# One ring of 40 rows, loads of eight rows and chains in fixed order, in a kernel that sums reciprocals

## The chip, the cores and the metric

The kernel runs on one core of one Trainium2 chip. The time is the device time of one execution in microseconds (us), as a median over several executions. Times inside a profile count from the start of its span, and the span is somewhat shorter than the measured time (172.6 against 175.2 us for the kernel before).

The engines are TensorE (PE in the profile; PEld is its weight load), VectorE (DVE), ScalarE (ACT), GpSimd (POOL) and SyncE (SP), which issues the DMAs.

## The reference

```python
x = np.abs(np.random.randn(32, 512, 1024)).astype(np.float32) + 1e-6
return np.sum(1.0 / x, axis=-1).astype(np.float32)
```

There are 16384 sums of 1024 reciprocals. With 128 partitions, each partition holds 128 "rows" of 1024 elements (4 KB); "a row" below means one row on all 128 partitions. All of x, 67.1 MB, has to be read once.

## The kernel before

The kernel takes reciprocals on ScalarE as exp(-ln x), and halves that work with an identity: for the two halves a and b of a row, 1/a + 1/b = (a + b) / (ab). So a product ab is made (512 elements), ScalarE takes Ln and Exp of it, and VectorE multiplies and sums. There are two ways to finish. In kind A VectorE multiplies both halves of the row by 1/(ab), a reduce over 1024 elements. In kind B TensorE first adds a + b into PSUM with an identity matrix, and VectorE reduces 512 elements only.

```python
A, B, C = (2, 0, GP, False), (2, 0, GP, True), (1, 1, GP, False)
GROUPS = (
    [A, B, A, B, C, B, A, B] * 7 + [A, B, A, B, A]
    + [(1, 0, GP, True), (1, 0, GP, False)] * 2
    + [(1, 0, GP, True), (1, 0, DV, True)]
)
...                                   # x tiles: 16 buffers of 2 rows
for np_, ns, eng, on_pe in GROUPS:
    xt = xpool.tile([P, n, D], f32, tag="xt")
    nc.sync.dma_start(out=xt, in_=x_v[:, c0 : c0 + n, :])
    eng.tensor_tensor(out=pr, in0=xt[:, :np_, :H], in1=xt[:, :np_, H:], op=mult)
    if on_pe:                         # kind B
        for j in range(np_):
            for h in range(2):
                nc.tensor.matmul(sm[:, j, :], lhsT=ident, rhs=xt[:, j, h*H:(h+1)*H],
                                 start=h == 0, stop=h == 1)
    ...                               # kind C: one row of two by ScalarE alone
    nc.scalar.activation(out=pr, in_=pr, func=Ln, scale=S)
    nc.scalar.activation(out=rc, in_=pr, func=Exp, scale=-1.0)
    for j in range(np_):
        nc.vector.tensor_tensor_reduce(out=row, in0=row, in1=rec, ..., accum_out=sums[...])
```

The order of the instructions on each engine is left to the scheduler of the framework. 64 of the 128 rows are of kind B.

Of the kernel before, what the change touches and what calls it, by code (L numbers as in the profile page):

```python
# [1 line left out]

# [6 lines left out]


@with_exitstack
def kernel(
    ctx: ExitStack,
    tc: tile.TileContext,
    x: bass.AP,
    out: bass.AP,
):








    nc = tc.nc
    f32 = mybir.dt.float32
    P = 128
    D = 1024
    H = D // 2  # L30
    F = 128

    S = float(2**17)



    GP, DV = nc.gpsimd, nc.vector
    A, B, C = (2, 0, GP, False), (2, 0, GP, True), (1, 1, GP, False)
    GROUPS = (
        [A, B, A, B, C, B, A, B] * 7  # L40
        + [A, B, A, B, A]
        + [(1, 0, GP, True), (1, 0, GP, False)] * 2
        + [(1, 0, GP, True), (1, 0, DV, True)]
    )

    Ln = mybir.ActivationFunctionType.Ln
    Exp = mybir.ActivationFunctionType.Exp
    mult = mybir.AluOpType.mult
    add = mybir.AluOpType.add

    x_v = x.flatten_outer_dims().rearrange("(p f) d -> p f d", p=P)
    out_v = out.flatten().rearrange("(p f) -> p f", p=P)

    act_sets = list(get_activation_tables(nc.m.arch).keys())
    nc.scalar.add_instruction(  # L55
        mybir.InstLoadActFuncSet(
            name=nc.get_next_instruction_name(),
            act_func_set_id=act_sets.index("natural_log_exp_and_others"),
            ins=[],
            outs=[],  # L60
        )
    )

    xpool = ctx.enter_context(tc.tile_pool(name="xpool", bufs=16))
    ppool = ctx.enter_context(tc.tile_pool(name="ppool", bufs=4))
    opool = ctx.enter_context(tc.tile_pool(name="opool", bufs=1))
    rpool = ctx.enter_context(
        tc.tile_pool(name="rpool", bufs=2, space=bass.MemoryType.PSUM)
    )

    spool = ctx.enter_context(
        tc.tile_pool(name="spool", bufs=2, space=bass.MemoryType.PSUM)
    )

    sums = opool.tile([P, F], f32)
    ident = opool.tile([P, P], f32)
    make_identity(nc, ident)

    c0 = 0
    for np_, ns, eng, on_pe in GROUPS:  # L80
        n = np_ + ns
        xt = xpool.tile([P, n, D], f32, tag="xt")
        nc.sync.dma_start(out=xt, in_=x_v[:, c0 : c0 + n, :])  # L83
        pr = ppool.tile([P, np_, H], f32, tag="pr")
        eng.tensor_tensor(out=pr, in0=xt[:, :np_, :H], in1=xt[:, :np_, H:], op=mult)  # L85
        if on_pe:
            sm = spool.tile([P, np_, H], f32, tag="sm")
            for j in range(np_):
                for h in range(2):
                    nc.tensor.matmul(  # L90
                        sm[:, j, :],
                        lhsT=ident,
                        rhs=xt[:, j, h * H : (h + 1) * H],
                        start=h == 0,
                        stop=h == 1,
                    )
        for j in range(np_, n):
            nc.scalar.activation(out=xt[:, j, :], in_=xt[:, j, :], func=Ln)  # L98
            nc.scalar.activation(  # L99
                out=xt[:, j, :],  # L100
                in_=xt[:, j, :],
                func=Exp,
                scale=-1.0,
                accum_out=sums[:, c0 + j : c0 + j + 1],
            )
        nc.scalar.activation(out=pr, in_=pr, func=Ln, scale=S)  # L106
        if on_pe:
            rc = pr
        else:
            rc = rpool.tile([P, np_, H], f32, tag="rc")  # L110
        nc.scalar.activation(out=rc, in_=pr, func=Exp, scale=-1.0)  # L111
        for j in range(np_):
            if on_pe:
                row, rec = rc[:, j, :], sm[:, j, :]
            else:
                row = xt[:, j, :].rearrange("p (h e) -> p h e", h=2)
                rec = rc[:, j, :].unsqueeze(1).to_broadcast([P, 2, H])
            nc.vector.tensor_tensor_reduce(  # L118
                out=row,
                in0=row,  # L120
                in1=rec,
                scale=S,
                scalar=0.0,
                op0=mult,
                op1=add,
                accum_out=sums[:, c0 + j : c0 + j + 1],
            )
        c0 += n
    assert c0 == F, c0

    nc.sync.dma_start(out=out_v, in_=sums)


# [1 line left out]
_INS = ['x']  # L135
_OUTS = [((32, 512), 'float32')]


# [23 lines left out]
```

## Time and profile before

The median is 175.2 us (174.65 to 175.26, three runs).

| engine | busy us of 172.6 | what it does |
|---|---|---|
| DMA | full from 4 to 160 us | loads of two rows, at the end one |
| GpSimd | 143.4 | 120 of 121 products (seven rows have none) |
| ScalarE | 142.0 | Ln and Exp |
| TensorE | 120.9 | sums of 64 rows |
| VectorE | 109.8 | reduces |

The prediction shows the lines. A line of a group gives count, busy time, mean duration in ns, and after the second bar the idle time before these instructions and what ended it.

### The profile page before, as it was taken

The numbers are of one execution on the slowest core, as the hardware profiler recorded it, in microseconds if no ns is written. First come the engines' busy times: TensorE is split into PE (matmuls) and PEld (weight loads), VectorE is DVE, ScalarE is ACT, GpSimd is POOL, SyncE is SP. The second block draws the span as 40 slices with busy tenths as digits, with TensorE's granted clock in tenths as the row PEclk, the third lists the DMA queues.
The fourth block names the chain that finished last, engine by engine and source line by source line (L and its number), as shares of the span: only waits on it lengthen the run. The fifth ranks groups of instructions, "written<-read, shape, count | busy, mean of one in ns | idle before, by whom it ended". The sixth has DMA issues, their size and how long they took to land.

```text
span 172.6 us, 1342 instructions
## 1 busy us (share of the span) xinstructions
PE 120.9 (70%) x256; PEld 47.4 (27%) x256; DVE 109.8 (64%) x243; ACT 142.0 (82%) x156; POOL 143.4 (83%) x72
## 2 busy tenths in 40 slices
PE   0099776767876767788666668977667876669480
PEld 0043322222332222233322223422222332223130
DVE  0009757874776757775578847468576755787791
ACT  2159989899878998889888996889988898988981
POOL 1599699969989799987999688997999979999920
PEclk9999999999999999999999996999999999999999
DMA  5999999999999999999999999999999999999500
GB/s 190 416 433 425 423 420 423 421 421 423 418 425 420 423 418 423 423 420 423 421 421 420 423 414 423 421 420 420 425 418 425 425 420 421 421 412 408 220 0 15
DMA packets 9799, 67.25 MB, mean 390 GB/s; under 512 B 1088, under 2 KB 1216, under 8 KB 1984
## 3 DMA queue, kind: packets, MB, share of 16 engines
q1 hardware_dynamic: 9792, 67.18, 94.0%
q8 instruction: 2, 0.03, 0.1%
q14 instruction: 5, 0.04, 0.1%
HBM read 67.11 MB, written 0.07 MB: 389 GB/s over the span
## 4 chain that ended last, share of the span: by engine, by line
DMA 78%; POOL 11%; ACT 2%; issue 2%; DVE 2%; SPq 1%; PE 1%; POOLq 0%; DVEq 0%
DMA xt<-in_x_dram 78%; POOL pr L85 11%; SPq L83 1%; ACT pr L106 1%; PE sm L90 1%; DVE xt L118 1%; ACT rc L111 1%; DVE pr L118 0%; ACT pr L111 0%; DVE pr L85 0%; POOLq L85 0%; DVE sums L118 0%; DVEq L118 0%; DVEq L157 0%
## 5 line engine op out<-in xcount | busy, mean ns | idle before, releaser
L85 POOL TENSOR_TENSOR pr<-xt 128x1024 f32<-128x1024 f32 (+1 forms) x66 | 142.7, 2166 | 21.1 <-DMA xt<-in_x_dram 15.2
L90 PE MATMUL sm<-xt,ident 128*128 128x512 f32 x256 | 120.9, 617 | 47.0 <-DMA xt<-in_x_dram 45.0
L118 DVE CUSTOM_DVE_ANT_1 xt<-xt,rc 128x1024 f32<-128x1024 f32 x57 | 67.7, 1219 | 50.2 <-issue 27.2
L106 ACT ACTIVATE pr<-pr 128x1024 f32<-128x1024 f32 (+1 forms) x67 | 65.0, 970 | 24.5 <-POOL pr L85 23.7
L90 PEld LDWEIGHTS sm<-xt,ident 128*128 128x128 f32 x256 | 47.4, 195 | 119.7 <-issue 57.8
L118 DVE CUSTOM_DVE_ANT_0 pr<-pr,sm 128x512 f32<-128x512 f32 x64 | 41.6, 685 | 9.8 <-ACT pr L111 8.6
L111 ACT ACTIVATE pr<-pr 128x1024 f32<-128x1024 f32 (+1 forms) x34 | 34.2, 1006 | 1.0
L111 ACT ACTIVATE rc<-pr 128x1024 f32<-128x1024 f32 (+1 forms) x33 | 29.9, 906 | 0.8
L118 DVE DVE_READ_ACCUMULATOR2_ANT sums<- 128x1 f32 x121 | 10.0, 82 | 0.0
L99 ACT ACTIVATE xt<-xt 128x1024 f32<-128x1024 f32 x7 | 7.3, 1041 | 0.0
L98 ACT ACTIVATE xt<-xt 128x1024 f32<-128x1024 f32 x7 | 7.3, 1040 | 0.0
L55 ACT ACT_TABLE_LOAD x1 | 1.3, 1283 | 0.7 <-PEq L146 0.7
L99 ACT ACTIVATION_READ_ACCUMULATOR xt<-xt 128x1 f32 x7 | 1.3, 186 | 0.0
L85 DVE TENSOR_TENSOR pr<-xt 128x512 f32<-128x512 f32 x1 | 0.7, 689 | 0.0
masks.py:197 POOL MEMSET ident<- 128x128 f32 x1 | 0.2, 204 | 0.3 <-POOLq L146 0.3
masks.py:199 POOL TENSOR_SCALAR_AFFINE_SELECT ident<-ident 128x128 f32<-128x128 f32 x1 | 0.3, 292 | 0.1
L146 POOL MEMSET const-float32-0.0<- 128x1 f32 x1 | 0.1, 98 | 0.2 <-issue 0.2
L146 POOL MEMSET const-bfloat16-1.0<- 128x1 bf16 x1 | 0.1, 101 | 0.0
L146 POOL MEMSET const-uint8-127<- 128x1 uint8 x1 | 0.1, 101 | 0.0
L146 POOL MEMSET const-float32-1.0<- 128x1 f32 x1 | 0.1, 98 | 0.0
## 6 DMA issues: line engine op xcount, KB each, us to landing
xt<-in_x_dram SPq DMA_DIRECT2D x61, 1024.0 KB, 19.8
xt<-in_x_dram SPq DMA_DIRECT2D x6, 512.0 KB, 15.6
out_dram<-sums SPq DMA_DIRECT2D x1, 64.0 KB, 1.5
```

The costliest lines, as they stand in the source:

```text
L55: nc.scalar.add_instruction(mybir.InstLoadActFuncSet(name=nc.get_next_instruction_name(), act_func_set_id=act_sets.index("natural_log_exp_ ...
L83: nc.sync.dma_start(out=xt, in_=x_v[:, c0 : c0 + n, :])
L85: eng.tensor_tensor(out=pr, in0=xt[:, :np_, :H], in1=xt[:, :np_, H:], op=mult)
L90: nc.tensor.matmul(sm[:, j, :], lhsT=ident, rhs=xt[:, j, h * H : (h + 1) * H], start=h == 0, stop=h == 1,)
L98: nc.scalar.activation(out=xt[:, j, :], in_=xt[:, j, :], func=Ln)
L99: nc.scalar.activation(out=xt[:, j, :], in_=xt[:, j, :], func=Exp, scale=-1.0, accum_out=sums[:, c0 + j : c0 + j + 1],)
L106: nc.scalar.activation(out=pr, in_=pr, func=Ln, scale=S)
L111: nc.scalar.activation(out=rc, in_=pr, func=Exp, scale=-1.0)
L118: nc.vector.tensor_tensor_reduce(out=row, in0=row, in1=rec, scale=S, scalar=0.0, op0=mult, op1=add, accum_out=sums[:, c0 + j : c0 + j + 1],)
L146: nc = _bacc.Bacc("TRN2", target_bir_lowering=False, num_devices=1)
```

## The change

The intent is to keep the stream of x denser (packets of 32 KB in place of 8 KB), to free GpSimd by giving 30 of the products to VectorE (GpSimd keeps 98 of 128, where it made 120), and to shorten the end by loads that shrink to one row. The order on every engine is fixed by hand. In the body a chain A of three rows and a chain B of four alternate; the last 30 rows are all of kind B. VectorE's products come in two kinds: for rows in V, TensorE copies one half into PSUM so that VectorE has one input only in SBUF; for rows in W, all in the tail, both inputs are in SBUF.

```diff
+    R = 40
+    LOADS = [8] * 11 + [5, 4, 3, 2, 5, 3, 3, 2, 3, 3, 1, 1, 2, 2, 1]
+    GROUPS = [(3, "A"), (4, "B")] * 14 + [(n, "B") for n in (4, 4, 4, 4, 4, 4, 3, 2, 1)]
+    V = {6 + 7 * i for i in range(14)} | {105, 108, 109}
+    W = {99, 101, 103, 104, 113, 115, 117, 118, 120, 121, 122, 123, 125}
...
+    ring = pool.tile([P, R, D], f32)
+    ps = pspool.tile([P, 8, H], f32)          # B: banks 0-3, A: 4-6, copies for V: 7
...
+    def product_v(g):
+        for r in range(g[0], g[0] + g[1]):
+            if r in V:
+                nc.tensor.matmul(ps[:, 7, :], lhsT=ident, rhs=xs(r, 1), start=True, stop=True)
+                b = ps[:, 7, :]
+            elif r in W:
+                b = xs(r, 1)
+            else:
+                continue
+            nc.vector.tensor_tensor(out=prod[:, p, :], in0=xs(r, 0), in1=b, op=mult)
...
+    with tc.manual_schedule():
+        for i, (r0, n, kind) in enumerate(chains):
+            ...                                # GpSimd's products of the chain
+            if kind == "A": rc = ps[:, 4 : 4 + n, :]
+            else:                              # B: two matmuls a row
+                tail = r0 >= 98
+                for j in range(n):
+                    bank[r0 + j] = nextb if tail else j
+                    for h in range(2): nc.tensor.matmul(ps[:, bank[r0 + j], :], ...)
+            nc.scalar.activation(out=pg, in_=pg, func=Ln, scale=S)
+            nc.scalar.activation(out=rc, in_=pg, func=Exp, scale=-1.0)
+            product_v(chains[i + 1])           # next chain's, before this one's reduces
+            ...                                # n reduces on VectorE
+            ahead(r0 + n)                      # loads for which the ring has room
```

More of the change, by code (lines that the diff above doesn't have):

```diff
@@ L31 @@
     F = 128
+    R = 40
+    NP = 20
     S = float(2**17)
-    GP, DV = nc.gpsimd, nc.vector
-    A, B, C = (2, 0, GP, False), (2, 0, GP, True), (1, 1, GP, False)
-    GROUPS = (
-        [A, B, A, B, C, B, A, B] * 7
-        + [A, B, A, B, A]
-        + [(1, 0, GP, True), (1, 0, GP, False)] * 2
-        + [(1, 0, GP, True), (1, 0, DV, True)]
-    )
+    LOADS = [8] * 11 + [5, 4, 3, 2, 5, 3, 3, 2, 3, 3, 1, 1, 2, 2, 1]
+    GROUPS = [(3, "A"), (4, "B")] * 14 + [(n, "B") for n in (4, 4, 4, 4, 4, 4, 3, 2, 1)]
+    V = {6 + 7 * i for i in range(14)} | {105, 108, 109}
+    W = {99, 101, 103, 104, 113, 115, 117, 118, 120, 121, 122, 123, 125}
     Ln = mybir.ActivationFunctionType.Ln
@@ L62 @@
     )
-    xpool = ctx.enter_context(tc.tile_pool(name="xpool", bufs=16))
-    ppool = ctx.enter_context(tc.tile_pool(name="ppool", bufs=4))
-    opool = ctx.enter_context(tc.tile_pool(name="opool", bufs=1))
-    rpool = ctx.enter_context(
-        tc.tile_pool(name="rpool", bufs=2, space=bass.MemoryType.PSUM)
-    )
-    spool = ctx.enter_context(
-        tc.tile_pool(name="spool", bufs=2, space=bass.MemoryType.PSUM)
-    )
-    sums = opool.tile([P, F], f32)
-    ident = opool.tile([P, P], f32)
@@ L77 @@
-    make_identity(nc, ident)
-    c0 = 0
-    for np_, ns, eng, on_pe in GROUPS:
-        n = np_ + ns
-        xt = xpool.tile([P, n, D], f32, tag="xt")
-        nc.sync.dma_start(out=xt, in_=x_v[:, c0 : c0 + n, :])
-        pr = ppool.tile([P, np_, H], f32, tag="pr")
-        eng.tensor_tensor(out=pr, in0=xt[:, :np_, :H], in1=xt[:, :np_, H:], op=mult)
-        if on_pe:
-            sm = spool.tile([P, np_, H], f32, tag="sm")
-            for j in range(np_):
-                for h in range(2):
-                    nc.tensor.matmul(
-                        sm[:, j, :],
-                        lhsT=ident,
-                        rhs=xt[:, j, h * H : (h + 1) * H],
-                        start=h == 0,
-                        stop=h == 1,
-                    )
-        for j in range(np_, n):
-            nc.scalar.activation(out=xt[:, j, :], in_=xt[:, j, :], func=Ln)
-            nc.scalar.activation(
-                out=xt[:, j, :],
-                in_=xt[:, j, :],
-                func=Exp,
-                scale=-1.0,
-                accum_out=sums[:, c0 + j : c0 + j + 1],
-            )
-        nc.scalar.activation(out=pr, in_=pr, func=Ln, scale=S)
-        if on_pe:
-            rc = pr
-        else:
-            rc = rpool.tile([P, np_, H], f32, tag="rc")
-        nc.scalar.activation(out=rc, in_=pr, func=Exp, scale=-1.0)
-        for j in range(np_):
-            if on_pe:
-                row, rec = rc[:, j, :], sm[:, j, :]
-            else:
-                row = xt[:, j, :].rearrange("p (h e) -> p h e", h=2)
-                rec = rc[:, j, :].unsqueeze(1).to_broadcast([P, 2, H])
-            nc.vector.tensor_tensor_reduce(
-                out=row,
-                in0=row,
-                in1=rec,
-                scale=S,
-                scalar=0.0,
-                op0=mult,
-                op1=add,
-                accum_out=sums[:, c0 + j : c0 + j + 1],
-            )
-        c0 += n
@@ L129, with load_one @@
-    assert c0 == F, c0
-    nc.sync.dma_start(out=out_v, in_=sums)
+    pool = ctx.enter_context(tc.tile_pool(name="pool", bufs=1))
+    pspool = ctx.enter_context(
+        tc.tile_pool(name="pspool", bufs=1, space=bass.MemoryType.PSUM)
+    )
+    ring = pool.tile([P, R, D], f32)
+    prod = pool.tile([P, NP, H], f32)
+    sums = pool.tile([P, F], f32)
+    ident = pool.tile([P, P], f32)
+    ps = pspool.tile([P, 8, H], f32)
+    loads = list(LOADS)
+    loaded = 0
+    def load_one():
+        nonlocal loaded
+        n = loads.pop(0)
+        r0 = loaded
+        a = r0 % R
+        m = min(n, R - a)
+        nc.sync.dma_start(out=ring[:, a : a + m, :], in_=x_v[:, r0 : r0 + m, :])
+        if m < n:
+            nc.sync.dma_start(
+                out=ring[:, 0 : n - m, :], in_=x_v[:, r0 + m : r0 + n, :]
+            )
+        loaded += n
@@ new lines, in need, with ahead @@
+    def need(r):
+        while loaded < r:
+            load_one()
+    def ahead(done):
+        while loads and loaded + loads[0] <= done + R:
+            load_one()
+    pslot = {}
+    nextp = 0
+    chains = []
+    r = 0
+    for n, kind in GROUPS:
+        if nextp + n > NP:
+            nextp = 0
+        for j in range(n):
+            pslot[r + j] = nextp + j
+        nextp = (nextp + n) % NP
+        chains.append((r, n, kind))
+        r += n
+    assert r == F and sum(LOADS) == F
@@ new lines, in xs, with pieces, product @@
+    def xs(r, h):
+        return ring[:, r % R, h * H : (h + 1) * H]
+    def pieces(r, n):
+        a = r % R
+        m = min(n, R - a)
+        return [(r, m)] + ([(r + m, n - m)] if m < n else [])
+    def product(r0, n):
+        for r, m in pieces(r0, n):
+            a, p = r % R, pslot[r]
+            nc.gpsimd.tensor_tensor(
+                out=prod[:, p : p + m, :],
+                in0=ring[:, a : a + m, :H],
+                in1=ring[:, a : a + m, H:],
+                op=mult,
+            )
@@ new lines, in product_v @@
+    def product_v(g):
+        for r in range(g[0], g[0] + g[1]):
+            p = pslot[r]
+            if r in V:
+                nc.tensor.matmul(
+                    ps[:, 7, :], lhsT=ident, rhs=xs(r, 1), start=True, stop=True
+                )
+                b = ps[:, 7, :]
[4 more added lines that the diff above has]
+            nc.vector.tensor_tensor(out=prod[:, p, :], in0=xs(r, 0), in1=b, op=mult)
+    make_identity(nc, ident)
@@ new lines @@
+    with tc.manual_schedule():
+        ahead(0)
+        product_v(chains[0])
+        nextb = 0
+        for i, (r0, n, kind) in enumerate(chains):
+            need(r0 + n)
+            r = a = r0
+            while r <= r0 + n:
+                if r == r0 + n or r in V or r in W:
+                    if r > a:
+                        product(a, r - a)
+                    a = r + 1
+                r += 1
+            p0 = pslot[r0]
+            pg = prod[:, p0 : p0 + n, :]
+            bank = {}
+            if kind == "A":
+                rc = ps[:, 4 : 4 + n, :]
+            else:
+                rc = pg
+                tail = r0 >= 98
+                for j in range(n):
+                    bank[r0 + j] = nextb if tail else j
+                    nextb = (nextb + 1) % 7 if tail else 0
+                    for h in range(2):
+                        nc.tensor.matmul(
+                            ps[:, bank[r0 + j], :],
+                            lhsT=ident,
+                            rhs=xs(r0 + j, h),
+                            start=h == 0,
+                            stop=h == 1,
+                        )
+            nc.scalar.activation(out=pg, in_=pg, func=Ln, scale=S)
+            nc.scalar.activation(out=rc, in_=pg, func=Exp, scale=-1.0)
+            if i + 1 < len(chains):
+                need(chains[i + 1][0] + chains[i + 1][1])
+                product_v(chains[i + 1])
+            for r in range(r0, r0 + n):
+                j = r - r0
+                if kind == "A":
+                    row = ring[:, r % R, :].rearrange("p (h e) -> p h e", h=2)
+                    rec = rc[:, j, :].unsqueeze(1).to_broadcast([P, 2, H])
+                else:
+                    row, rec = pg[:, j, :], ps[:, bank[r], :]
+                nc.vector.tensor_tensor_reduce(
+                    out=row,
+                    in0=row,
+                    in1=rec,
+                    scale=S,
+                    scalar=0.0,
+                    op0=mult,
+                    op1=add,
+                    accum_out=sums[:, r : r + 1],
+                )
+            ahead(r0 + n)
+        nc.sync.dma_start(out=out_v, in_=sums)
```

## The prediction

> **What bounds the kernel now.** I read the shares by slice first, because averages hide where an engine is full. In the page's second part each digit is the busy tenth of one 4.3 us slice:
>
> ```profile
> ACT  2159989899878998889888996889988898988981
> POOL 1599699969989799987999688997999979999920
> ...
> DMA  5999999999999999999999999999999999999500
> GB/s 190 416 433 425 423 420 423 421 421 423 418 425 420 423 418 423 423 420 423 421 421 420 423 414 423 421 420 420 425 418 425 425 420 421 421 412 408 220 0 15
> ```
>
> The DMA row has no gap between the second slice and the 37th: the stream of x is the bound of the body. GpSimd (POOL) and ScalarE (ACT) are close behind it. The rate falls in the last slices. The stretches say why:
>
> ```profile
> 0.00:4.00 4.00, 0.00 (x0) 0.00 (x0) 0.00 (x0) 1.28 (x1) 0.70 (x6) 1.00 0.55 172
> ...
> 60.00:80.00 20.00, 14.80 (x34) 5.87 (x33) 13.55 (x30) 17.74 (x20) 17.60 (x9) 1.00 1.01 422
> ...
> 155.00:160.00 5.00, 4.66 (x11) 1.59 (x9) 3.68 (x8) 4.22 (x5) 4.90 (x3) 1.00 1.02 408
> 160.00:165.00 5.00, 2.74 (x6) 1.17 (x7) 3.82 (x7) 4.88 (x8) 5.00 (x5) 1.00 0.42 164
> 165.00:170.00 5.00, 2.95 (x7) 0.87 (x5) 4.04 (x11) 3.18 (x6) 0.07 (x1) 1.00 0.00 0
> ```
>
> The columns are length, busy time of PE, PE's weight loads, VectorE (DVE), ACT and POOL, clock, DMA share, GB/s. The queues are full in both 60:80 and 155:160, but loads of two rows (8 KB to a partition) move 422 GB/s, the closing loads of one row (4 KB) only 408. The first stretch moved 172 x 4 = 0.69 MB, 1.6 us at 422, so bytes flow from about 2.4 us; the stretch 160:165 moved 0.82 MB, so they stop at about 162.0. Everything after that is tail. The chain that ended last says who fills it:
>
> ```profile
> 119.17 19.82 DMA xt<-in_x_dram
> ...
> 139.14 2.37 POOL pr L85
> ...
> 156.52 2.39 POOL pr L85
> 158.91 0.02 issue
> 158.93 1.07 ACT pr L106
> ...
> 169.09 0.69 DVE pr L118
> ```
>
> Up to 139 the chain is all loads; from 139 to 159 it is one GpSimd product after another: GpSimd is late by some microseconds when the stream ends, then ACT and VectorE work the rest off until 169.8. From there to the end of the span, 172.6, is the store of the sums and the close: 2.8 us. So before is start 2.4, stream 159.6, tail 7.8, close 2.8. The measured time is 175.2, 2.6 above the span, and I carry that 2.6 over.
>
> Costs of one instruction, from the groups kept apart by shape:
>
> ```profile
> L85 POOL TENSOR_TENSOR pr<-xt 128x1024 f32<-128x1024 f32 x54 | 127.6, 2365 | 20.3 <-DMA xt<-in_x_dram 15.0 <-ACT pr L106 1.1
> ...
> L106 ACT ACTIVATE pr<-pr 128x1024 f32<-128x1024 f32 x54 | 57.0, 1055 | 23.7 <-POOL pr L85 23.7
> ...
> L85 POOL TENSOR_TENSOR pr<-xt 128x512 f32<-128x512 f32 x12 | 15.1, 1273 | 0.7 <-DMA xt<-in_x_dram 0.2
> ...
> L106 ACT ACTIVATE pr<-pr 128x512 f32<-128x512 f32 x13 | 8.0, 615 | 0.8 <-DVE pr L85 0.8
> ```
>
> A product of GpSimd costs 181 ns and 1092 ns a row (2365 - 1273); an activation 175 ns and 440 ns a row. In the timeline VectorE starts its reduces 1.14 us apart where the row is the full one of 1024 (kind A), 0.61 us where it is 512 (kind B), and its own product takes 0.61 too.
>
> **What the Trainium skill says.** "DMA: Bandwidth & Descriptors", section "Specifications", gives 435 GB/s as the ceiling of the SBUF side; its section "Why small descriptors are slow" has a fixed overhead per packet inside the DMA engine. The trace agrees with both: 16 engines at 408 and 422 GB/s spend 160.6 ns on a 4 KB packet and 310.6 ns on an 8 KB one, so 150.0 ns for 4 KB and 10.6 ns fixed, which tends to 437 GB/s. "SBUF — State Buffer", section "Who interferes with whom": a VectorE instruction with two SBUF inputs and a GpSimd instruction that reads SBUF exclude one another, whichever started first runs to its end; with one SBUF input there is no conflict. That explains why 14 + 3 of the new products fetch one half through PE into PSUM. No line before shows the exclusion: the one VectorE product there runs at 167.0, when GpSimd has finished. "ScalarE: Activation LUTs", section "What ACT_TABLE_LOAD costs", has 186 ns + 0.833 ns an element, 1039 ns for 1024; the trace has 1055.
>
> **The change, part by part.**
>
> 1. Loads. 67 loads become 27 (26 in the list, of which rows 118 to 120 wrap round the ring and split). A load of n rows gives each of 16 engines 8 packets: n x 8 x 150.0 ns + 8 x 10.6 ns = 1.20 n + 0.085 us. Before: 128 x 1.20 + 67 x 0.085 = 159.3 us, which is the observed 159.6. After: 153.6 + 27 x 0.085 = 155.9. Gain 3.4 us, all of it on the path. Bytes would then end at 2.4 + 155.9 = 158.3. The first load of the kernel before was ready about 0.6 us after its bytes were due (5.5 against 2.4 + 2.5), so the last row is usable at 158.9.
>
> 2. The body. The first eight rows are usable only at 12.7 instead of the first two at 5.5. That costs nothing if the engines are faster than the stream. Seven rows (A of 3, B of 4) take the stream 8.5 us. GpSimd now makes six of the seven in two instructions of 0.18 + 3 x 1.09 = 3.46: 7.1 us with gaps, where it had almost no room. ACT: Ln and Exp of three rows 1.50 each, of four 1.94 each: 6.9. VectorE: 3 x 1.14 + 4 x 0.61 + 0.61 = 6.5. PE: 9 matmuls some 0.46 us apart, 4.1. All have 17% or more to spare. The seven rows whose sums ACT made alone are gone.
>
> 3. The ring. A load of eight needs the rows 40 before it released. Row 7 heads the third chain: its rows 8 and 9 land at 22.4, product to 25.9, Ln and Exp to 28.9, first reduce to 30.1. The sixth load can go then and is needed at 51.6, when the fifth ends. The second release comes at some 41 for 61. About 20 us are to spare, so the stream isn't starved.
>
> 4. The tail. I lay out the last chains with the landing time 3.0 + 1.20 rows + 0.085 loads. VectorE's order matters: the products of the next chain stand before the reduces of this one. Times in us; the third column is when the last product of the chain is ready:
>
> ```
> rows      landed  products  ACT to  reduces to
> 106-109   136.4   139.5     143.7   146.1
> 110-113   142.6   143.6     147.6   150.0
> 114-117   146.3   147.6     151.5   154.4
> 118-121   151.4   152.0     155.9   158.3
> 122-124   155.1   156.4     159.4   161.2
> 125-126   157.6   158.9     161.5   162.7
> 127       158.9   160.2     162.7   163.5
> ```
>
> For example 118-121: row 121 lands at 151.4, VectorE's product is done at 152.0, ACT needs 2 x 1.94, to 155.9, four reduces to 158.3. ACT then goes from chain to chain without a gap from 156.4: 3.0 + 2.1 + 1.25 for 3, 2 and 1 rows. To this I add 1.0 us as an estimate for the exclusion above: 113 beside the product of 110-112, 117 beside 116, 122/123 beside 124 and 125 beside 126 each may wait up to one GpSimd product, but some of it falls into waits that are there anyway. End of work 164.5, that is 5.6 after the last row instead of 7.2 (169.8 - 162.6).
>
> Sum: 164.5 + 2.8 = 167.3 span, + 2.6 = 169.9. Against 175.2 that is -5.3: 3.4 from packets, the rest from the tail. I put 169.8.
>
> **Rivals.** (a) Large packets don't pay: the rate stays 422 because something other than the packet cost sets it. For: the rate has been flat at 420 to 425 for 140 us, and only a stretch of 5 us shows 408. Against: the fit ends within half a per cent of the skill's ceiling, and the slice at 9 to 13 us shows 433. Then the loads end 3.4 later: 173.3, no change by the 2% rule. (b) The exclusion or VectorE's fixed order makes the tail the bound: a product that waits for a late row blocks the finished reduces behind it, and 13 products with two SBUF inputs take turns with GpSimd. VectorE has 3.1 to 4.3 us of work for each four rows against 4.9 of stream, so a wait of over 1 us per chain adds up. That would give back 2 to 4 us: 172 to 174. (c) The loads starve: if rows are released much later than in part 3, each eight-row load shows a gap in the DMA row. The 20 us speak against it; if it did happen at most of the 11 releases with 1 us each, 178 or more. (d) The tail is better than laid out, no exclusion felt: 168.5.
>
> **Range and chances.** Packets pay with some 75%; the tail is uncertain by 2 us either way. Main branch 168 to 172, rival (a) 172 to 174.5, (c) a few per cent above. The 2% lines are 171.7 and 178.7. So faster 0.71, same 0.25, slower 0.04; 167.3 to 173.2 should hold it 8 times in 10.
>
> **What will show it.** GB/s in the body should be 431 to 434, with no empty slice of DMA; if it is 420 to 425, step 1 is wrong. GpSimd should be busy for 98 products, near 112 us, and no longer a run of 20 us in the chain; the chain should be loads up to about 155 and then ACT and VectorE. The last load should land near 159 and work end near 164.5. VectorE's products in the tail with a mean well over 0.7 us, or products of GpSimd of one row well over 1.27, would show the exclusion. A chain with ring releases in it (a load waiting for VectorE) would make the prediction wrong upwards; so would a load lowered to packets of under 8 KB.

## More of the kernel before

One line that the prediction did not use, and should have, is TensorE's group (the view of groups of the kernel before, kept apart by shape):

```profile
L90 PE MATMUL sm<-xt,ident 128*128 128x512 f32 x256 | 120.9, 617 | 47.0 <-DMA xt<-in_x_dram 45.0 <-DVE sums L118 1.9
```

## The result

The changed kernel takes 197.07 us (196.77 to 197.23, four runs) against 174.93 of the kernel before in the same rounds. The ratio is 1.127, with a 95% interval of 1.124 to 1.130. A ratio here is the mean time of one kernel's fast runs over that of the other's of the same rounds, so it is not quite the ratio of the medians quoted. The prediction, 169.8 and faster with 71%, was wrong.

The second part of the page of the changed kernel, in slices of 4.9 us:

```profile
PE   0019988888896949999999989999999899999992
...
POOL 1029494999499949494949999994474244000000
...
DMA  6999999999999999999999999999999960000000
GB/s 222 430 430 430 437 437 444 430 437 430 445 430 430 427 437 430 430 430 430 437 425 430 403 423 425 427 434 411 415 428 411 424 271 0 2 3 0 0 0 13
```

The stream did what was hoped: no slice is empty, the rate is 427 to 445 up to 97 us where it was 416 to 433, and the bytes end in the 33rd slice, by estimate at about 159 us (271 / 424 of a slice that starts at 156). The last load is complete at 161.1 (landings and single records are read here from the kept trace, where no line is shown). GpSimd is done by 163. But TensorE is full to the end. The end of the chain that ended last reads (start, duration, what):

```profile
113.78 7.13 PE ps L161 x16
120.92 0.86 PE ps L124 x2
121.77 6.87 PE ps L161 x16
...
129.50 13.73 PE ps L161 x32
...
153.72 37.78 PE ps L161 x88
...
191.63 0.69 DVE prod L180
```

From 113.8 to 191.5 the chain is practically nothing but matmuls. L161 is the sum of a kind B row, L124 the copy for a V row. Sixteen records take 6.87 us, so one takes 0.43 us, and four B rows are sixteen records: four records a row. The piece of 32 records is rows 94 to 101; read record by record, the first one of row 98 starts at 136.2. The groups say the same:

```profile
L161 PE MATMUL ps<-ring,ident 128*128 128x512 f32 x344 | 151.1, 595 | 3.0 <-DVE sums L180 3.0
L124 PE MATMUL ps<-ring,ident 128*128 128x512 f32 x34 | 19.0, 642 | 21.6 <-DMA ring<-in_x_dram 20.8 <-DVE prod L132 0.8
```

The program issues 172 and 17 matmuls here; the trace has 344 and 34 records. Every matmul here, of 32-bit data, is two records. The line of the kernel before shows it as well: 256 records for 64 rows. The mean of 595 ns is longer than the 430 ns from start to start because matmuls overlap.

TensorE's account closes: 151.1 + 19.0 of busy time overlap to 166.9 us, idle time is 3.0 + 21.6, and the sum 191.5 is where the last matmul ends. Two stretches, before and after, show the body (columns as in the prediction):

```profile
60.00:100.00 40.00, 29.59 (x66) 11.66 (x65) 27.03 (x60) 35.55 (x39) 35.81 (x17) 1.00 1.01 422
```

```profile
60.00:100.00 40.00, 35.68 (x83) 15.41 (x82) 31.05 (x70) 30.29 (x20) 30.70 (x10) 1.00 1.00 431
```

ScalarE and GpSimd fell from 89 and 90% to 76 and 77%, as intended, and TensorE rose from 74% to 89%.

### The profile page after: what moved, and what is told of

Same layout as the page of the kernel before. It is cut to its first block, busy times and chain, and to the rows that moved or that the text cites. A ratio compares the mean times of both kernels' runs of the same rounds, so it can differ in the third digit from the quotient of the medians.

```text
span 195.0 us, 1440 instructions
## 1 busy us (share of the span) xinstructions
PE 166.9 (86%) x378; PEld 71.3 (37%) x378; DVE 123.5 (63%) x286; ACT 124.0 (64%) x75; POOL 114.6 (59%) x46
## 4 chain that ended last, share of the span: by engine, by line
DMA 45%; PE 40%; POOL 7%; issue 3%; DVE 2%; ACT 1%; SPq 0%; POOLq 0%; DVEq 0%; ACTq 0%
DMA ring<-in_x_dram 45%; PE ps L161 37%; POOL prod L113 7%; PE ps L124 3%; DVE ring L180 1%; ACT prod L168 1%; DVE prod L132 1%; DVE prod L180 1%; SPq L72 0%; DVE sums L180 0%; POOLq L113 0%; DVEq L180 0%; DVEq L132 0%; ACTq L168 0%; DVEq L217 0%
## 5 line engine op out<-in xcount | busy, mean ns | idle before, releaser
L161 PE MATMUL ps<-ring,ident 128*128 128x512 f32 x344 | 151.1, 595 | 3.0 <-DVE sums L180 3.0
L113 POOL TENSOR_TENSOR prod<-ring 128x1536 f32<-128x1536 f32 (+2 forms) x40 | 113.9, 2873 | 47.9 <-DMA ring<-in_x_dram 39.7
L168 ACT ACTIVATE prod<-prod 128x2048 f32<-128x2048 f32 (+3 forms) x37 | 62.0, 1676 | 60.0 <-DVE prod L132 31.3
L161 PEld LDWEIGHTS ps<-ring,ident 128*128 128x128 f32 x344 | 65.4, 191 | 87.5 <-issue 76.1
L180 DVE CUSTOM_DVE_ANT_0 prod<-prod,ps 128x512 f32<-128x512 f32 x86 | 55.3, 684 | 25.6 <-PE ps L161 12.3
L180 DVE CUSTOM_DVE_ANT_1 ring<-ring,ps 128x1024 f32<-128x1024 f32 x42 | 49.0, 1216 | 11.7 <-ACT ps L169 11.7
L169 ACT ACTIVATE prod<-prod 128x2048 f32<-128x2048 f32 (+3 forms) x23 | 41.4, 1799 | 0.7
L124 PE MATMUL ps<-ring,ident 128*128 128x512 f32 x34 | 19.0, 642 | 21.6 <-DMA ring<-in_x_dram 20.8
L132 DVE TENSOR_TENSOR prod<-ring,ps 128x512 f32<-128x512 f32 x17 | 11.6, 685 | 31.5 <-PE ps L124 31.5
L169 ACT ACTIVATE ps<-prod 128x1536 f32<-128x1536 f32 x14 | 20.4, 1455 | 0.4
L124 PEld LDWEIGHTS ps<-ring,ident 128*128 128x128 f32 x34 | 5.9, 196 | 31.8 <-issue 23.7
L180 DVE DVE_READ_ACCUMULATOR2_ANT sums<- 128x1 f32 x128 | 10.5, 82 | 0.0
L132 DVE TENSOR_TENSOR prod<-ring 128x512 f32<-128x512 f32 x13 | 9.5, 767 | 0.0
```

Of the source, the lines that this page charges most:

```text
L113: nc.gpsimd.tensor_tensor(out=prod[:, p : p + m, :], in0=ring[:, a : a + m, :H], in1=ring[:, a : a + m, H:], op=mult,)
L124: nc.tensor.matmul(ps[:, 7, :], lhsT=ident, rhs=xs(r, 1), start=True, stop=True)
L132: nc.vector.tensor_tensor(out=prod[:, p, :], in0=xs(r, 0), in1=b, op=mult)
L161: nc.tensor.matmul(ps[:, bank[r0 + j], :], lhsT=ident, rhs=xs(r0 + j, h), start=h == 0, stop=h == 1,)
L168: nc.scalar.activation(out=pg, in_=pg, func=Ln, scale=S)
L169: nc.scalar.activation(out=rc, in_=pg, func=Exp, scale=-1.0)
```

## The experiments

Twelve kernels ran. The theory after the result is that TensorE sets the end: from row 98 on it has 120 records for 30 rows and 6 for three copies, 126 x 0.43 = 54.1 us, while the prediction's layout had it all done in 40. The rivals are VectorE's fixed order, the exclusion between VectorE and GpSimd, and the large loads.

### e1: half of the tail's matmuls (a wrong result on purpose)

```diff
-                    for h in range(2):
+                    for h in range(1 if tail else 2):
...
-                            stop=h == 1,
+                            stop=tail or h == 1,
```

> Wrong result on purpose: in the last 30 rows PE adds up only one half of a row, so one matmul instead of two; every other instruction stays. Theory (PE's matmuls set the end: 126 records of 0.43 us from row 98 on): 60 records fewer, 25.8 us of PE; the end should come 20 to 26 us earlier, some 171 to 177 us, and PE should no longer be the long last piece of the chain. Rival (VectorE's fixed order and the exclusion between VectorE and GpSimd hold up the tail): PE was only waiting along, the time stays at 190 or above.

Measured: 176.44 us, 20.6 less than the changed kernel, within the range of the theory. The result was wrong (relative error 0.19). The first part of the page of the changed kernel, then of this one:

```profile
PE 166.9 (86%) x378; PEld 71.3 (37%) x378; DVE 123.5 (63%) x286; ACT 124.0 (64%) x75; POOL 114.6 (59%) x46
```

```profile
PE 143.8 (82%) x318; PEld 60.9 (35%) x318; DVE 122.4 (70%) x286; ACT 124.0 (71%) x75; POOL 114.6 (66%) x46
```

Only TensorE's line changed, by 60 records; every other engine has the same instructions in the same order, and they finish 20 us earlier. This shows that TensorE's matmuls in the tail cost at least 20 us.

### e2: the products with two SBUF inputs go back to GpSimd

```diff
-    W = {99, 101, 103, 104, 113, 115, 117, 118, 120, 121, 122, 123, 125}
+    W = set()
```

> The 13 products that VectorE makes in the tail with both inputs in SBUF go back to GpSimd; PE's work is the same. Theory (PE): 197 us within 1.5, although GpSimd does 13 products more and VectorE 13 fewer. Rival (exclusion): 3 us or more faster.

Measured: 196.99 us, no change. The exclusion is not what cost the time. It does exist: in the changed kernel's timeline one pair of VectorE products runs beside GpSimd (start, duration, engine, line).

```profile
160.07 2.99 POOL L113 TENSOR_TENSOR prod<-ring 128x512 f32<-128x512 f32 x2 [1.19 <-DMA ring<-in_x_dram]
...
161.24 2.36 DVE L132 TENSOR_TENSOR prod<-ring 128x512 f32<-128x512 f32 x2
```

The two VectorE products take 2.36 us where two take 1.29 alone, and the two of GpSimd 2.99 where two take some 2.55. The longest single one has 1.756 us in the trace, the median 0.686. Over all 13 the mean is 767 ns against 685 for those with one SBUF input, so 13 x 0.082 = 1.1 us in all. All of it lies in that single product (1.756 - 0.686 = 1.07): one of 13 waited, and here behind TensorE.

### e3: kinds A and B in turn to the end

```diff
-    GROUPS = [(3, "A"), (4, "B")] * 14 + [(n, "B") for n in (4, 4, 4, 4, 4, 4, 3, 2, 1)]
+    GROUPS = [(3, "A"), (4, "B")] * 17 + [(3, "A"), (3, "B"), (2, "A"), (1, "B")]
...
-                tail = r0 >= 98
+                tail = False
```

> The tail goes on with chains of kind A and B in turn, as in the body; products as in the change. B rows in the tail fall from 30 to 16: 56 PE records fewer, 24 us; VectorE pays 14 x 0.53 = 7.4 us more. Theory (PE): PE is done near 168, then VectorE, with some 35 us of work from about 137 on, sets the end: 174 to 181 us measured. Rival (order and exclusion): VectorE has more to do, so 197 or slower.

Measured: 183.34 us (182.49 to 184.49), 13.7 less, with a correct result. That is 2.3 above the range, but in the direction that only the theory has: VectorE does more, and the kernel is faster. The chain of this run changes hands in the tail:

```profile
149.62 8.91 PE ps L161 x16
...
160.37 1.75 DVE prod L132
162.12 1.13 DVE ring L180
```

Up to 158.5 it is TensorE, but for 3.7 us of VectorE from 143.8 on; after that it is VectorE. One reason for the miss is in the first of these lines: 16 records took 8.91 us in place of 6.87, and the granted clock was 0.82 between 150 and 160.

### e7: e3 without products of two SBUF inputs

```diff
     (e3, and)
+    W = set()
```

> e3_tail_mixed with the 13 VectorE products of two SBUF inputs given to GpSimd. There VectorE was the last engine to be busy, from 159 on without a gap. If VectorE's load and the exclusion count once PE is no longer the bound: 13 x 0.61 = 7.9 us of VectorE fewer and some 1 us of exclusion, so 174 to 178 us. If PE still sets the end in e3_tail_mixed: 182 to 184, no change, as in e2.

Measured: 177.92 us, 5.4 less than e3, in the range for "VectorE counts". The same edit was worth nothing in e2 and 5.4 us here. What an engine's work costs depends on who is the bound.

### e4: no copies for VectorE in the body

```diff
-    V = {6 + 7 * i for i in range(14)} | {105, 108, 109}
+    V = {105, 108, 109}
```

> In the body GpSimd makes all products, so PE copies no rows for VectorE there: 14 matmuls, 28 records, 12.0 us of PE fewer; GpSimd gets 14 rows more (7.9 us of 8.4 per seven rows). Theory (PE is the bound already in the body, with a backlog of some 12 us at row 98): 183 to 188 us. Rival (only the tail is bound by PE, the body keeps up with the stream): 195 to 198, no change.

Measured: 200.39 us, 3.3 slower than the changed kernel. Both expectations missed. TensorE has 28 records fewer, and the tail is still as long. The stretch from 80 to 100 us of this run shows where the time was taken back:

```profile
80.00:100.00 20.00, 17.58 (x37) 7.64 (x38) 14.59 (x36) 17.43 (x11) 20.00 (x6) 0.91 1.01 434
```

GpSimd is busy for all of the 20 us. With all products of the body it became the last in line, as the chain shows; its last line is the sums of rows 98 to 101.

```profile
118.00 7.97 POOL prod L113 x2
126.00 1.92 ACT prod L168
...
139.42 7.13 PE ps L161 x16
```

These sums start at 139.4, 3.2 us later than in the changed kernel. After its start at 13.5 TensorE never waited for a load, but 13 times, 21.2 us in all, for banks that VectorE had yet to read. So taking work from TensorE in the body helps nothing if GpSimd then fills up. What the copies by themselves cost is not shown by this run, because the edit put another engine in their place.

### e12: the changed kernel with the loads of before

```diff
-    LOADS = [8] * 11 + [5, 4, 3, 2, 5, 3, 3, 2, 3, 3, 1, 1, 2, 2, 1]
+    LOADS = [2] * 61 + [1] * 6
```

> The changed kernel with the loads of the kernel before (61 of two rows, 6 of one), nothing else. If PE's 54 us of work from row 98 on set the end, the loads hardly matter: 194 to 198 us, and PE again the last long piece of the chain. If the loads of eight rows are what cost the 22 us: below 185.

Measured: 195.39 us, and the chain again ends in one piece of 37.78 us of TensorE. The large loads account for 1.7 us of the loss at most; with TensorE as the bound they gained nothing.

### e5 and e6: balanced chains, with large and with small loads

e5 keeps the ring, the loads and the fixed order and takes chains A of four and B of three rows:

```diff
-    GROUPS = [(3, "A"), (4, "B")] * 14 + [(n, "B") for n in (4, 4, 4, 4, 4, 4, 3, 2, 1)]
-    V = {6 + 7 * i for i in range(14)} | {105, 108, 109}
-    W = {99, 101, 103, 104, 113, 115, 117, 118, 120, 121, 122, 123, 125}
+    GROUPS = [(4, "A"), (3, "B")] * 17 + [(2, "B"), (2, "A"), (2, "B"), (1, "A"), (1, "B"), (1, "B")]
+    V = {6 + 7 * i for i in range(17)} | {126}
+    W = set()
...
-                rc = ps[:, 4 : 4 + n, :]
+                rc = ps[:, 3 : 3 + n, :]
...
-                tail = r0 >= 98
+                tail = False
```

> Same ring, loads and fixed order, but chains A of 4 and B of 3 rows to the end, one VectorE product (through PE) in seven rows, none with two SBUF inputs, small chains at the very end. Counted in records as the chip runs them, PE has 12 + 2 of 0.43 us, 6.0 us, per seven rows; VectorE 7.0, ACT 6.9, GpSimd 7.1, the stream 8.4. Theory (the change lost to PE's load): the stream is the bound again, 167 to 171 us, faster than before by 2 to 4.5%. Rival (the ring, the large loads or the fixed order cost time themselves): 175 or slower although PE is relieved.

e6 is e5 with `LOADS = [2] * 61 + [1] * 6`.

> e5_balanced with the loads of the kernel before: 61 of two rows and 6 of one. Theory (a packet costs 10.6 ns besides its bytes): 67 loads instead of 27, 40 x 0.085 = 3.4 us slower than e5_balanced, 422 instead of 430 to 436 GB/s. Rival (packets don't matter for the end, or the early start of compute with small loads pays it back): within 1 us of e5_balanced.

Measured: 182.82 us for e5 and 180.90 for e6 (ratios to before 1.045 and 1.034, intervals apart). Both expectations for the theory missed: e5 is 12 us above its range, and e6 is faster than e5, not slower. No engine is over 75% busy in e5, yet the stream is not the bound. The waits of e5 (total us, times, longest):

```profile
ACT prod L168 <- POOL prod L113: 38.2, 10, 16.0
...
DVE ring L180 <- ACT ps L169: 25.7, 9, 5.7
...
PE ps L161 <- DVE sums L180: 23.6, 13, 4.4
```

Each engine waits for another: TensorE for banks that VectorE has yet to read, ScalarE for GpSimd (16.0 of it at the start), VectorE for ScalarE. I read this as chains of four rows, with one set of banks for each kind, that make the engines take turns; no run tests this alone. My sums per seven rows had no term for it. The granted clock was also lower, 0.91 in the profiles of e5 and e6 against 0.99 and more in the changed kernel's runs; what that cost is not separated.

### e10: e7 with the loads of before

```diff
     (e7, and)
+    LOADS = [2] * 61 + [1] * 6
```

> e7_tail_mixed_no_w (177.9 us, PE busy without a gap from 113 to 165 us) with loads of two rows and at the end one. If eight-row loads cost PE time in the body (first matmul at 13.7 us, and idle until the next eight rows land), then PE starts 8 us earlier and it ends 3 to 8 us earlier, 170 to 175. If the shorter stream counts: 3.4 us slower, 181.

Measured: 178.30 us (ratio 1.021; e7 has 1.017, from other rounds). Neither range holds it, and no difference from e7 can be told. TensorE did not start 8 us earlier but at 13.03: in the fixed order its first instruction is the copy for row 6, and that needs the fourth load of two rows. In the tail it stands idle, as the timeline shows (the bracket has the idle time before it and what ended it):

```profile
147.95 2.08 PE L124 MATMUL ps<-ring,ident 128*128 128x512 f32 x2 [3.48 <-DVE prod L132]
```

The copies for 108 and 109 share one bank with each other, so the second waits until VectorE has used the first.

### e8 and e9: the kernel before with larger loads

One part of the change alone. Rows 6 to 117 are loaded by fours (e8) or eights (e9), the others from six small buffers; everything else is as before.

```diff
-    xpool = ctx.enter_context(tc.tile_pool(name="xpool", bufs=16))
+    xpool = ctx.enter_context(tc.tile_pool(name="xpool", bufs=8))       # e9: 4
+    xspool = ctx.enter_context(tc.tile_pool(name="xspool", bufs=6))
+    BIG = 4                                                             # e9: 8
...
+        if 6 <= c0 < 118:
+            o = (c0 - 6) % BIG
+            if o == 0:
+                xb = xpool.tile([P, BIG, D], f32, tag="xb")
+                nc.sync.dma_start(out=xb, in_=x_v[:, c0 : c0 + BIG, :])
+            xt = xb[:, o : o + n, :]
...                                    # the other rows as before, from xspool
```

> The kernel before with one part of the change alone: 28 loads of four rows in place of 56 of two, rows 6 to 117; the chains, engines and order stay as they were. 28 x 0.085 = 2.4 us of stream fewer. If the size of the loads pays at the end: 172 to 173.5 us. Rival (GpSimd, over 90% busy there, and rows that land later in lumps take it back): 174.5 to 176.

> The same with 14 loads of eight rows: 42 x 0.085 = 3.6 us of stream fewer, 430 GB/s or more. If the size of the loads pays at the end: 171 to 172.5 us. Rival (lumps of eight rows leave GpSimd idle until they land and late afterwards): 175 or slower, slower than with loads of four.

Measured: e8 174.11 us (ratio 0.996, interval 0.994 to 0.998) and e9 179.32 (ratio 1.026). From 60 to 100 us the rate is 422 GB/s before, 427 in e8 and 431 in e9, so the packets pay in the stream, as the fit said; at the end of e8 they bring half a microsecond of the 2.4, and in e9 the rival is right. GpSimd's timeline of the kernel before, then of e9:

```profile
119.25 18.66 POOL L85 TENSOR_TENSOR pr<-xt 128x1024 f32<-128x1024 f32 x8 [1.23 <-DMA xt<-in_x_dram]
139.14 25.92 POOL L85 TENSOR_TENSOR pr<-xt 128x1024 f32<-128x1024 f32 x13 [1.23 <-DMA xt<-in_x_dram]
```

```profile
138.48 8.25 POOL L94 TENSOR_TENSOR pr<-xb 128x1024 f32<-128x1024 f32 x4 [0.38 <-DMA xb<-in_x_dram]
148.19 9.32 POOL L94 TENSOR_TENSOR pr<-xb 128x1024 f32<-128x1024 f32 x4 [1.46 <-DMA xb<-in_x_dram]
157.48 7.17 POOL L94 TENSOR_TENSOR pr<-xt 128x1024 f32<-128x1024 f32 x4
165.21 3.75 POOL L94 TENSOR_TENSOR pr<-xt 128x512 f32<-128x512 f32 x3 [0.56 <-ACT rc L120]
```

With loads of eight, GpSimd starts on eight rows only when the last of them has landed, and needs about as long for them (8.3 to 9.3 us) as the stream for the next eight (9.7). So it stays one load behind for the whole run: it ends at 169.0 where it ended at 165.1 before. In e8 it ends at 164.8, as before. My edit has a flaw of its own: the last loads also waited for one of the six small buffers, and in e9 the last two were issued only at 163.1. GpSimd's only gap after 148.2, though, is 0.56 us, for ScalarE, and no engine is seen to wait for these two loads, so in e9 no cost of the flaw is seen; in e8 it may have eaten part of the gain, which is left open. In e9 the granted clock was lower too, 0.91 in its profile against 0.98 to 1.00 before; GpSimd's products took their usual 2.4 us, and what the clock cost elsewhere is not separated.

### e11: chains of three, a load for each chain

A version meant to beat both.

```diff
-    R = 40
+    R = 39
-    LOADS = [8] * 11 + [5, 4, 3, 2, 5, 3, 3, 2, 3, 3, 1, 1, 2, 2, 1]
+    LOADS = [3] * 41 + [2, 1, 1, 1]
-    GROUPS = [(3, "A"), (4, "B")] * 14 + [(n, "B") for n in (4, 4, 4, 4, 4, 4, 3, 2, 1)]
+    GROUPS = [(3, "A"), (3, "B")] * 20 + [(3, "A"), (2, "B"), (1, "A"), (1, "B"), (1, "B")]
-    V = {6 + 7 * i for i in range(14)} | {105, 108, 109}
+    V = {3 + 6 * i for i in range(21)}
-    W = {99, 101, 103, 104, 113, 115, 117, 118, 120, 121, 122, 123, 125}
+    W = set()
...
-                    bank[r0 + j] = nextb if tail else j
-                    nextb = (nextb + 1) % 7 if tail else 0
+                    bank[r0 + j] = nextb
+                    nextb = (nextb + 1) % 4
```

> A version meant to beat both: a ring of 39 rows, one load for each chain of three rows (small ones at the end), chains A and B of three in turn to the end, sums in four banks in rotation, VectorE's product through PE is the first row of each B chain, none with two SBUF inputs. Per six rows: PE 14 records, 6.0 us; GpSimd 6.0; ACT 6.0; VectorE 5.9; stream 7.4. If the lessons hold (no engine over 85%, and what is landed in one piece is no larger than what one chain takes): the stream is the bound, bytes end at 2.4 + 153.6 + 45 x 0.085 = 159.8, the last row needs 4 us, 169 to 171 us measured, 2 to 3.5% faster than before. If the fixed order itself costs time: 175 or slower.

Measured: 175.08 us, ratio 1.002 (1.000 to 1.003): level with the kernel before, and 22 us faster than the changed one with the same ring, the same fixed order and the same kind of VectorE product. The shares of its chain by engine:

```profile
DMA 90%; POOL 3%; DVE 2%; issue 2%; POOLq 1%; ACT 0%; SPq 0%; DVEq 0%
```

The stream is the bound again, so a ring and a fixed order need not make the kernel slower than before. My 169 to 171 missed by the tail: the last load of three rows landed at 157.0, and GpSimd then made five products in a row until 165.5, where I had counted 4 us after the last row. e11 changed chain size, banks, place of the copy and loads together, so which of these freed it from the turns of e5 isn't separated.

The version that beats both is e8, by 0.4% over the kernel before.

## Why the prediction was wrong

The step that failed is in its part 2: "PE: 9 matmuls some 0.46 us apart, 4.1". The duration was about right for a record (0.43), but the count was of matmuls in the program, where the trace has two records for each. Per seven rows TensorE has 16 + 2 records, 7.7 us of the stream's 8.5, not 4.1. The conclusion "all have 17% or more to spare" was false for it, and in the tail, part 4, TensorE was not laid out at all. There it has 54.1 us of work, where the layout ran from row 98's landing, 124.2 by its formula, to 164.5, 40.3 us. The group line of the kernel before, 256 records for 64 rows, would have shown it.

The Trainium skill would have too. "FP8 and Floating Point Precision", section "TensorE Precision Notes", says that true FP32 takes four passes through the array. "TensorE: Matmul & The Clock Gate", Part 1 (on the HAM clock gate), has 215.7 ns from start to start for 512 columns when warm, so four passes are estimated at 863 ns. The trace agrees: a matmul of the changed kernel, two records, takes 0.86 us.

The sum of the miss: work ended at 192.3, not 164.5, 27.8 us later. TensorE began on row 98 at 136.2, 12.0 us after 124.2. From there to its last matmul, at 191.5, it took 55.3 us, 15.0 more than the layout's 40.3: the 54.1 of its records, 0.8 of waiting for the bank of the copies, and 0.4 of longer records where a piece starts or ends. The last reduce adds 0.8. That the tail's matmuls cost this time is shown by e1 and e3, and e12 shows that it is not the large loads.

Of the 12.0 us, 2.3 are that row 98 landed at 126.5 and not at 124.2. The other 9.7 are a backlog of TensorE. Its first matmul starts at 13.7 because of the eight-row load, and its 252 records up to row 98 make 108.4. In between it is idle for 10.1: six waits for a load, 7.1 in all, and four for banks that VectorE had yet to read, 3.0. The 4.0 still missing to 136.2 are slower records; the first two of the run, for one, took 2.05 us. In TensorE's order the copy for the last row of a B chain stands before all sums of that chain, so these wait until the whole chain has landed, whatever the size of a load: with loads of two rows (e12) TensorE waits 8.9 us for loads after its start at 13.2, and begins on row 98 at 135.1. In e4, without these copies, waits for banks took the place of the waits for loads. Which of these waits counts most is left open.

TensorE's load is also not the whole distance to 169.8. With half of the tail's sums left out (e1) the kernel still took 176.4, and no run with the ring came under the 175.1 of e11. So it is not shown that the prediction would have held with TensorE counted rightly.

The other steps, one by one:

- Loads (part 1): the rate was right. 431 GB/s from 60 to 100 us where 431 to 434 was expected, bytes end at 159.1 by estimate (158.3), no empty slice. Rival (a) is refuted. The landings were put too early: the last load was complete at 161.1, not 158.9, and in the kernel before at 164.0, not 162.6, so the gain was 2.9 us, not 3.4. That it would be "all of it on the path" was wrong: in the changed kernel it is hidden behind TensorE, in e9 the later landing of the lumps took it back, and in e8 0.5 us of the expected 2.4 was left.
- First rows usable at 12.7: the first product started at 13.6. "That costs nothing if the engines are faster than the stream" failed for engines that are only just faster: TensorE here, at 91% (7.7 of 8.5), and GpSimd in e9, 89% busy from 60 to 100 us.
- Durations: three rows on GpSimd 3.463 us (3.46), Ln of three and four rows 1.474 and 1.912 (1.50, 1.94), VectorE as expected. GpSimd's 98 products took 113.9 us (112). Right.
- The ring (part 3): right. The sixth load went out at 31.2 (30.1), and the fifth was complete at 52.6 (51.6; the formula itself gives 51.4). Rival (c) did not occur.
- Exclusion: the size, 1.1 us against 1.0, was met by luck. The prediction shared it among four places; it was one wait, of row 117's product beside GpSimd's of row 127, which was none of them, and it lay beside TensorE and cost nothing (e2). Rival (b) is refuted as the cause of the loss: e2 takes the exclusion away, e1 keeps VectorE's order and is 20.6 us faster. VectorE's products do count once TensorE is relieved (e7).

No rival named TensorE, and the range of 167.3 to 173.2 had no room for an engine that was not laid out.

## What to carry to other kernels

When work is moved onto an engine that was not the bound, count that engine's work in the unit in which the profile counts it, records and their distance from start to start, and lay it out for the tail as well as for the body. Larger loads made the stream itself faster (422 to 431 GB/s here), but rows can be used only when the whole load has landed; an engine that is nearly full stays that much behind until the end. Dividing busy time by rows gives only a lower bound for chains that go through four engines: banks and buffers decide whether they overlap.

## What the Trainium skill lacked or had wrong

- "TensorE: Matmul & The Clock Gate" has no figure for 32-bit matmuls, and no page says that a trace holds two records for one of them; 172 matmuls gave 344 records here, 0.43 us apart, 0.86 us for 512 columns.
- "SBUF — State Buffer", section "The DMA setup-cost knee", advises the largest single transfer one can make. The section says that the semaphore fires only after the last byte, but does not weigh that against the advice: loads of eight rows in the kernel before raised the rate from 422 to 431 GB/s and made it 2.6% slower, loads of four gave 427 GB/s and 0.4% faster.
- "SBUF — State Buffer", section "Who interferes with whom", was borne out: a VectorE product with two SBUF inputs took 1.756 us beside a GpSimd product in place of 0.686. What the section lacks is how often that happens; here it was one of 13 such products.
